# Seven block products instead of eight in the first MLP matmul, and a scheduler that keeps TensorE's array shape

## The chip, the cores and the metric

The kernel runs on one core of a Trainium2 chip, whose engines work side by side: TensorE (PE, with PEld for its weight loads), VectorE (DVE), ScalarE (ACT), GpSimd (POOL), and SyncE (SP), which issues the DMA transfers. The metric is the device time of one execution in microseconds, as the median of several runs; lower is better.

## The reference

One layer of a bidirectional RWKV-7 / GLA backbone for 256 context tokens and 2048 latent tokens of width 1024: a modulated RMSNorm, an input projection, two recurrent mixers, an output projection with a gated residual, and then what the change touches:

```python
    x = x + gt1 * o
    h = _rmsnorm(x, p['norm2_g']) * (1.0 + sc2) + sh2
    f = jnp.square(jax.nn.relu(h @ p['mlp_w1'])) @ p['mlp_w2']
    x = x + gt2 * f
    return x, new_states
...
    y_prompt = _rmsnorm(xp, final_norm_g)
    y_sample = _rmsnorm(xs, final_norm_g)
```

`mlp_w1` is 1024 x 4096 and `mlp_w2` 4096 x 1024, in float32. The gate `gt2` has one row for the context tokens and one for the latent tokens.

## The kernel before

Every large float32 product is made of three fast ones: an operand is split into a high part (ScalarE casts it) and a low part (VectorE subtracts the high part), and `mm3` issues high x high, high x low and low x high into one PSUM bank. A "triple" below is such a group.

The kernel has three stages. `proj` makes the input projection, with small matmuls of other array shapes between its triples (rows with `hh`, `hl`, `w_hi`, `w_lo` are the triples; rows `Q`, `K` belong to the GLA heads). `mixers` runs the scans. `tail` makes the output projection, the second norm and the MLP.

In each stage the program first records its instructions in a `Plan`; then `Plan.order` and `Plan.lay` set the order in which they are emitted on each engine. A recorded operation has a cost in the plan's own units, and its urgency is the cost of the longest chain behind it. `lay` goes through time, takes for each engine the most urgent operation that is ready, and hands out PSUM banks and work tiles as they come free. All emitted instructions carry the line number of that one loop (L534 in the profile before), so tiles are told apart by name and not by line.

The tail works on 18 units of 128 tokens, in the order of `UNITS`: units 9 and 10 hold the context tokens. `Tail.unit` makes the output projection of a unit (tiles `woh`, `wol`, and `h2h`, `h2l` for the mixer output), adds the residual, stores it (`d_x`), normalises and transposes it into `h2`. The split `h2` of nine units lies in SBUF in `h2h` and `h2l`; six of the eight blocks of units 9 to 16 and all of unit 17 go there directly, and the rest through DRAM (`d_h`) and `reload`.

`mlp(u0)` is called for units 9 to 17 and then for 0 to 8. Each pass has 16 groups (`gi`) of 256 hidden columns. A group loads two blocks of 128 columns of `mlp_w1` (tile `w1r`, split into `woh`, `wol`) and the matching rows of `mlp_w2` (`w2r`); makes for each 128 hidden columns and each 384 tokens a product over 8 blocks of the inner dimension, 24 matmuls of 384 columns into a bank `ps_1`; takes it through ReLU, square and split (`rr`); and multiplies with `mlp_w2`, 6 matmuls of 512 columns into a bank `ps_2` per 128 tokens and half width, which VectorE adds to `acc`. From group `PRE` = 13 on the gate is applied: `acc` is multiplied by `gt`, the residual is added, and the last two groups multiply their products by the gate before adding. In group 15 the final norm follows and the rows are stored.

The names `woh`, `wol` in the MLP's rows are the weights and hidden values, since all of these share those tiles.

## Time and profile before

| what | value |
|---|---|
| median of 3 runs | 3704.69 us (3702.34 to 3711.63) |
| profiled execution | 3709.88 us, span 3708.2 us |
| mean granted clock of TensorE | 0.963 |
| input projection | 0 to about 1280 us |
| mixers | about 1280 to 1810 us |
| units of the tail | about 1830 to 2085 us |
| MLP | about 2085 us to the end |
| DMA moved | 411.47 MB |

Times are microseconds unless marked ns. A row of the timeline gives start, duration, engine, line, operation, output <- inputs, shape and count, and in brackets the idle time before it and what ended it. A row of groups gives count, busy time, mean ns of one, and the idle time before. Matmuls overlap their successors, so a matmul's price is the distance between starts. A form such as 128*64 is the part of the array that a matmul uses.

### The profile page before, as it was taken

What the parts mean: (1) busy time and instruction counts of PE and PEld (TensorE: products, weight loads), DVE (VectorE), ACT (ScalarE), POOL (GpSimd) and SP (SyncE); (2) the same over time, 40 slices, a digit from 0 to 9 for tenths busy, and PEclk for the clock granted to TensorE, in tenths of its full rate; (3) what the DMA queues carried; (4) which work ended last, traced back from release to release, by engine and by line L of the source; (5) the groups of instructions that cost most, each with busy time, mean ns of one, the idle gap of its engine ahead of it and who ended that gap; (6) DMA issues with size and microseconds to landing.
All of it is one profiled execution on the core that took longest, in us unless ns stands there. A gap on an engine that the chain in (4) does not pass through costs nothing.

```text
span 3708.2 us, 74382 instructions
## 1 busy us (share of the span) xinstructions
PE 3504.4 (95%) x28927; PEld 3104.1 (84%) x28927; DVE 2249.8 (61%) x4991; ACT 1871.6 (50%) x4264; POOL 200.7 (5%) x500
## 2 busy tenths in 40 slices
PE   6999999999999779999699999999999999999998
PEld 4989888977888668888587899999999899999997
DVE  2665778756888778788487534334447734444357
ACT  5566857775568567788567622222223422222222
POOL 1111002200011210100000000000000000000000
PEclk8999999999999889899799999999999999999999
DMA  5356335532245655565688411111114311111122
GB/s 170 110 152 172 103 84 167 145 107 56 62 129 160 181 159 168 154 193 164 168 250 248 146 40 46 35 40 46 46 43 136 130 34 46 46 46 40 46 70 101
DMA packets 504207, 411.47 MB, mean 111 GB/s; under 512 B 87761, under 2 KB 458926, under 8 KB 503854
## 3 DMA queue, kind: packets, MB, share of 16 engines
q1 hardware_dynamic: 503854, 406.71, 37.6%
q8 instruction: 228, 3.74, 0.4%
q14 instruction: 125, 1.02, 0.1%
HBM read 287.03 MB, written 119.55 MB: 110 GB/s over the span
## 4 chain that ended last, share of the span: by engine, by line
PE 46%; DMA 2%; DVE 1%; ACT 1%; issue 0%; DVEq 0%; SPq 0%; ACTq 0%
PE ps L534 46%; DVE acc L534 1%; DMA hf<-d_h 0%; ACT hf L534 0%; DMA xb<-in_w_out_dram 0%; DVE xb L534 0%; DMA xa<-in_x_sample_dram 0%; DVE h2l L534 0%; DMA d_h<-hf 0%; DMA xb<-in_x_sample_dram 0%; DMA acc<-in_x_prompt_dram 0%; DMA xa<-in_x_prompt_dram 0%; ACT xb L534 0%; ACT h2h L534 0%; DVE gf L534 0%
## 5 line engine op out<-in xcount | busy, mean ns | idle before, releaser
L534 DVE TENSOR_TENSOR acc<-acc,ps 128x512 f32<-128x512 f32 x468 | 319.8, 688 | 504.0 <-PE ps L534 503.5
L534 PE MATMUL ps<-hh,w_hi 128*128 128x384 f32 (+3 forms) x1736 | 594.2, 342 | 5.2 <-ACT w_hi L534 3.9
L534 PE MATMUL ps<-hh,w_lo 128*128 128x384 f32 (+3 forms) x1736 | 548.7, 316 | 0.9 <-DVE w_lo L534 0.9
L534 PE MATMUL ps<-hl,w_hi 128*128 128x384 f32 (+3 forms) x1736 | 549.0, 316 | 0.0
L534 ACT ACTIVATE rr<-ps 128x384 f32<-128x384 f32 x192 | 94.4, 492 | 869.2 <-PE ps L534 861.5
L534 PE MATMUL ps<-h2l,woh 128*128 128x384 f32 x1536 | 516.4, 336 | 0.6 <-DVE h2l L534 0.4
L534 PE MATMUL ps<-h2h,woh 128*128 128x384 f32 x1536 | 513.9, 335 | 0.9 <-ACT h2h L534 0.9
L534 PE MATMUL ps<-h2h,wol 128*128 128x384 f32 x1536 | 514.1, 335 | 0.0
L534 PE MATMUL ps<-woh,wol 128*128 128x512 f32 x1152 | 456.2, 396 | 0.0
L534 PE MATMUL ps<-wol,woh 128*128 128x512 f32 x1152 | 454.0, 394 | 0.0
L534 PEld LDWEIGHTS ps<-hh,w_hi 128*128 128x128 f32 (+1 forms) x1736 | 328.4, 189 | 39.1 <-issue 10.3
L534 PEld LDWEIGHTS ps<-hl,w_hi 128*128 128x128 f32 (+1 forms) x1736 | 329.0, 190 | 2.9 <-DVE hl L534 0.4
L534 PEld LDWEIGHTS ps<-hh,w_lo 128*128 128x128 f32 (+1 forms) x1736 | 327.9, 189 | 3.4 <-DVE w_lo L534 1.7
L534 PEld LDWEIGHTS ps<-h2l,woh 128*128 128x128 f32 x1536 | 288.3, 188 | 23.3 <-DVE h2l L534 1.6
L534 PEld LDWEIGHTS ps<-h2h,woh 128*128 128x128 f32 x1536 | 288.4, 188 | 21.2 <-ACT h2h L534 1.6
L534 PE MATMUL ps<-woh,woh 128*128 128x512 f32 x774 | 301.1, 389 | 0.5 <-ACT woh L534 0.5
L534 PEld LDWEIGHTS ps<-h2h,wol 128*128 128x128 f32 x1536 | 288.3, 188 | 0.0
L534 DVE TENSOR_TENSOR wol<-rr,woh 128x384 fp32r<-128x384 f32 x192 | 103.7, 554 | 267.4 <-ACT woh L534 267.4
L534 PEld LDWEIGHTS ps<-woh,wol 128*128 128x128 f32 x1152 | 215.9, 187 | 46.7 <-DVE wol L534 0.9
L534 PEld LDWEIGHTS ps<-wol,woh 128*128 128x128 f32 x1152 | 215.9, 187 | 31.2
L534 ACT CAST woh<-rr 128x384 fp32r<-128x384 f32 x192 | 95.7, 515 | 201.4 <-PE ps L534 198.4
L534 PEld LDWEIGHTS ps<-woh,woh 128*128 128x128 f32 x774 | 145.4, 188 | 21.5 <-ACT woh L534 0.8
(296 smaller groups left out, 6735.7 us busy)
## 6 DMA issues: line engine op xcount, KB each, us to landing
w_raw<-in_w_in_dram SPq DMA_DIRECT2D x72, 512.0 KB
w1r<-in_mlp_w_dram SPq DMA_DIRECT2D x64, 512.0 KB
w2r<-in_mlp_w_dram SPq DMA_DIRECT2D x64, 512.0 KB
BK<-d_bk SPq DMA_DIRECT2D x36, 512.0 KB
AR<-d_ar SPq DMA_DIRECT2D x72, 256.0 KB
acc<-d_yo SPq DMA_DIRECT2D x36, 512.0 KB
w_raw<-in_ada_w_dram SPq DMA_DIRECT2D x32, 512.0 KB
d_ar<-s SPq DMA_DIRECT2D x56, 256.0 KB
```

What stands on the lines that cost most here:

```text
L534: getattr(getattr(self.nc, eng), method)(*[at(x) for x in args], **{k: at(x) for k, x in kw.items()})
```

## The change

Two things are changed.

**The MLP.** Its passes are three, over units 0 to 5, 12 to 17 and 6 to 11, 768 tokens each. All of `h2` goes through DRAM. Per group the first product is seen as a 2 x 2 block product: `mlp_w1`'s 256 columns in two halves, its 1024 rows in two halves, the tokens in two halves of 384. The Strassen-Winograd scheme replaces its eight block products by seven, each of 12 matmuls of 384 columns (4 blocks of the inner dimension, 3 each). `reload` forms the seven operands from `h2` once a pass: four blocks as loaded, and t1, t2, t3 and one further difference, each split high and low into `h2h`, `h2l`; VectorE and GpSimd share this. For the first pass it runs in two halves, since three of the operands lie where the output projection's weights were. `blocks` forms the four weight sums in place in `w1r` and in `s1`, splits seven operands, and adds the products in SBUF (tile `q`) before ReLU, square and split. In the two passes with a single gate row, `mlp_w2`'s rows are multiplied by the gate and the residual is loaded into `acc` at the start. The pass over units 6 to 11 has both gate rows and keeps the old scheme; it is last. PSUM turns of the tail change from three and two to five and three for `ps_1` and `ps_2`.

**The scheduler.** Each TensorE operation has an array shape (rows and columns rounded up to 32, 64 or 128). Where the most urgent ready one has another shape than the last one emitted, `lay` takes a ready one of the same shape whose urgency is less than `PW` = 2.0 behind, if its tiles are free. This holds in all three stages.

```diff
+PW = 2.0
...
-BK_TAIL = [2, {"ps_t": 3, "ps_h": 1, "ps_m": 3, "ps_1": 3, "ps_2": 2}]
+BK_TAIL = [2, {"ps_t": 3, "ps_h": 1, "ps_m": 3, "ps_1": 5, "ps_2": 3}]
...
             i = heapq.heappop(can[e])[1]
+            if e == "tensor" and self.shape[i] != shape:
+
+                for x in sorted(y for y in can[e] if y[0] < -prio[i] + PW and self.shape[y[1]] == shape):
+                    new = [y for y in self.held[x[1]].values() if y.ap is None]
+                    if not short(new) and all(min(idle[y.kind.name])[0] <= t for y in new):
+                        can[e].remove(x)
+                        can[e].append((-prio[i], i))
+                        heapq.heapify(can[e])
+                        i = x[1]
+                        break
...
-        self.h = [tp.tile([128, 8, 1152], F32R, name=f"h2{x}") for x in "hl"]
+        self.h = [tp.tile([128, 7, 4, 384], F32R, name=f"h2{x}") for x in "hl"]
...
-            k0 = 4 * i
-            k1 = k0 + 4 if u == 17 else min(k0 + 4, 8 - MR) if u >= 9 else k0
...
-            for k in range(k1, k0 + 4):
-                nc.sync.dma_start(out=d.h2[128 * k:128 * k + 128, us], in_=hf[:, k - k0])
+            for j in range(4):
+                k = 4 * i + j
+                nc.sync.dma_start(out=d.h2[128 * k:128 * k + 128, us], in_=hf[:, j])
...
+        def both(k, i, x):
+            hi, lo = [y[:, i, k] for y in self.h]
+            nc.scalar.copy(hi, x)
+            eng = nc.gpsimd if i in (1, 5, 6) else nc.vector
+            eng.tensor_tensor(out=lo, in0=x, in1=hi.bitcast(F32), op=ALU.subtract)
+        for k in range(4):
+            b11, t3, b22, b21 = load(k, 0, 0), load(k, 0, 1), load(k, 1, 1), load(k, 1, 0)
+            t1 = self.next(b)
+            TT(out=t1, in0=t3, in1=b11, op=ALU.subtract)
+            both(k, 0, b11)
+
+            t2 = self.next(b)
+            TT(out=t2, in0=b22, in1=t1, op=ALU.subtract)
+            nc.gpsimd.tensor_tensor(out=t3, in0=b22, in1=t3, op=ALU.subtract)
+            both(k, 2, t2)
+            both(k, 1, b21)
+            both(k, 3, t3)
+            if not first:
+                TT(out=b21, in0=b21, in1=t2, op=ALU.subtract)
+                both(k, 4, t1)
+                both(k, 5, b21)
+                both(k, 6, b22)
...
+        def part(w, b):
+            wh, wl = self.next("w1")
+            split(g, wh, wl, w)
+            ps = self.ps.tile([128, 512], F32, name="ps_1")[:, 0:384]
+            for k in range(4):
+                mm3(g, ps, wh[:, k], wl[:, k], self.h[0][:, b, k], self.h[1][:, b, k], k == 0, k == 3)
+            return ps
...
+        u1 = self.next("u")
+        nc.scalar.copy(u1, part(a11, 0))
+        TT(out=s1, in0=a21, in1=a22, op=ALU.add)
+        TT(out=a21, in0=a11, in1=a21, op=ALU.subtract)
+        TT(out=a11, in0=s1, in1=a11, op=ALU.subtract)
+        u2 = add("u", u1, part(a11, 2))
+        out(0, 0, add("r", u1, part(a12, 1)))
+        u3 = add("u", u2, part(a21, 3))
+        p5 = part(s1, 4)
+        out(1, 1, add("r", u3, p5))
+        TT(out=u2, in0=u2, in1=p5, op=ALU.add)
+        TT(out=s1, in0=a12, in1=a11, op=ALU.subtract)
+        out(1, 0, add("r", u3, part(a22, 5)))
+        out(0, 1, add("r", u2, part(s1, 6)))
...
+        if one:
+            self.gate(grp[0], 1)
+            for i in turn:
+                residual(i, acc[i])
...
+                if one:
+                    TT(out=raw, in0=raw, in1=self.gt, op=ALU.mult)
...
-        t.mlp(9)
-        for k in range(8):
-            for u0 in (0, 3, 6):
-                t.reload(k, u0, 3)
-        t.mlp(0)
+        for u0 in (0, 12, 6):
+            t.reload(u0, u0 == 0)
+            t.mlp(u0)
```

Three places show how the emitted order moves. The first is PE in the input projection, in the last third of its triples. Before:

```order
L534 MATMUL ps_120<-Q_188,K_214 64x64 x4
L534 MATMUL ps_119<-hh,w_hi_200 128x384
L534 MATMUL ps_119<-hl,w_hi_200 128x384
L534 MATMUL ps_119<-hh,w_lo_202 128x384
L534 MATMUL ps_125<-Q_189,K_215 64x64 x4
```

With the change, at the same place among the triples:

```order
L562 MATMUL ps_121<-hl,w_hi_199 128x384
L562 MATMUL ps_121<-hh,w_lo_201 128x384
L562 MATMUL ps_126<-Q_189,K_215 64x64
L562 MATMUL ps_124<-Q_188,K_214 64x64 x4
L562 MATMUL ps_126<-Q_189,K_215 64x64 x3
L562 MATMUL ps_121<-hh,w_hi_199 128x384
L562 MATMUL ps_121<-hl,w_hi_199 128x384
L562 MATMUL ps_121<-hh,w_lo_201 128x384
L562 MATMUL ps_123<-hh,w_hi_200 128x384
```

Two small groups of one shape, each of which stood alone between triples, now stand together. The second place is DVE in a steady MLP group. Before, accumulations and splits alternate, with one split of 1024 columns per weight block:

```order
L534 TENSOR_TENSOR wol_21711<-w1r,woh_21710 128x1024
L534 TENSOR_TENSOR wol_21713<-rr,woh_21712 128x384
L534 TENSOR_TENSOR acc_21717<-acc_21717,ps_21740 128x512
L534 TENSOR_TENSOR acc_21717<-acc_21717,ps_21735 128x512
L534 TENSOR_TENSOR acc_21717<-acc_21717,ps_21738 128x512
L534 TENSOR_TENSOR acc_21717<-acc_21717,ps_21739 128x512
```

With the change (`q` with `ps` is a sum of block products, `s` and `w1r` without a low part are weight sums, `w2r` with `gt` is the gate):

```order
L562 TENSOR_TENSOR wfl<-w1r,wfh 128x512 x3
L562 TENSOR_TENSOR wfl<-s_21714,wfh 128x512
L562 TENSOR_TENSOR s_21714<-w1r 128x512
L562 TENSOR_TENSOR acc<-acc,ps_21727 128x512
L562 TENSOR_TENSOR acc<-acc,ps_21729 128x512
L562 TENSOR_TENSOR acc<-acc,ps_21733 128x512
L562 TENSOR_TENSOR q<-q,ps_21730 128x384
L562 TENSOR_TENSOR wfl<-w2r,wfh 128x1024
L562 TENSOR_TENSOR wfl<-w1r,wfh 128x512
L562 TENSOR_TENSOR q<-q,ps_21728 128x384
```

Between the accumulations there are now sums out of PSUM and of weights, and more and smaller splits. The third place is DVE where the first pass meets the second. It stands there now:

```order
L562 TENSOR_TENSOR q<-xb,q 128x384
L562 TENSOR_TENSOR xa<-q 128x384
L562 TENSOR_TENSOR q<-q 128x384
L562 TENSOR_TENSOR q<-q,xa 128x384
L562 TENSOR_TENSOR h2l<-xa,h2h 128x384
L562 TENSOR_TENSOR acc<-acc,ps_21728 128x512
L562 TENSOR_TENSOR acc<-acc,ps_21734 128x512
L562 TENSOR_TENSOR acc<-acc,ps_21733 128x512
L562 TENSOR_TENSOR wfl<-w2r,wfh 128x1024
L562 TENSOR_TENSOR h2l<-q,h2h 128x384 x2
```

Rows of `q`, `xa`, `xb` without `ps` are operand differences, and `h2l` rows are their splits. Before, where the two passes met, only splits stood in this place, between gate products:

```order
L534 TENSOR_TENSOR h2l<-hf,h2h 128x384
L534 TENSOR_TENSOR acc_21714<-acc_21714,xb 128x512
L534 TENSOR_TENSOR wol_21713<-rr,woh_21712 128x384 x2
L534 TENSOR_TENSOR wol_21711<-w2r,woh_21710 128x1024
L534 TENSOR_TENSOR h2l<-hf,h2h 128x384 x2
L534 TENSOR_TENSOR wol_21711<-w1r,woh_21710 128x1024
```

More of the change, by code (lines that the diff above doesn't have):

```diff
@@ L445, in lay, with short @@
         step = -1 if back else 1
+        def short(new):
+            for x in new:
+                if len(idle[x.kind.name]) <= (0 if x.n == turn[x.kind.name] else x.kind.spare):
+                    return x
         cur, self.nsw = None, 0
+        shape, self.nshape = None, 0
         engs = ("tensor", "vector", "scalar", "gpsimd", "sync")
@@ L472, in lay @@
             i = heapq.heappop(can[e])[1]
+            if e == "tensor" and self.shape[i] != shape:
[7 more added lines that the diff above has]
+                        break
             new = [x for x in self.held[i].values() if x.ap is None]
-            lack = [x for x in new if len(idle[x.kind.name]) <= (0 if x.n == turn[x.kind.name] else x.kind.spare)]
+            lack = short(new)
             if lack:
-                stuck[lack[0].kind.name].setdefault(lack[0].n, []).append(i)
+                stuck[lack.kind.name].setdefault(lack.n, []).append(i)
                 continue
@@ L500, in lay @@
             t = max(t, ready[i])
+            if e == "tensor":
+                if self.shape[i] != shape:
+                    pass
+                    self.nshape += 1
+                shape = self.shape[i]
             free[e] = t + busy
@@ L1571, in __init__ @@
         halves = lambda x: [x[:, 0:512], x[:, 512:1024]]
+        cut = [q[:, 384 * i:384 * i + 384] for i in range(8)]
         self.rings = {
[L1573 to L1576 removed]
@@ new lines, in reload, with load @@
+    def reload(self, u0, first=False):
+        g = self.g
+        nc, TT = g.nc, g.nc.vector.tensor_tensor
+        b = "b0" if first else "b"
+        def load(k, i, j):
+            r0, c0 = 128 * (4 * i + k), 128 * (u0 + 3 * j)
+            x = self.next(b)
+            nc.sync.dma_start(out=x, in_=g.d.h2[r0:r0 + 128, c0:c0 + 384])
+            return x
+        def both(k, i, x):
[19 more added lines that the diff above has]
+                both(k, 6, b22)
+        b = "b1"
+        for k in range(4) if first else ():
+            b11, t1, b22, t4 = load(k, 0, 0), load(k, 0, 1), load(k, 1, 1), load(k, 1, 0)
+            TT(out=t1, in0=t1, in1=b11, op=ALU.subtract)
+            both(k, 4, t1)
+            TT(out=t4, in0=t4, in1=b22, op=ALU.subtract)
+            both(k, 6, b22)
+            TT(out=t4, in0=t4, in1=t1, op=ALU.add)
+            both(k, 5, t4)
@@ new lines, in blocks, with add, out @@
+    def blocks(self, gi):
+        g = self.g
+        nc, TT = g.nc, g.nc.vector.tensor_tensor
+        w1 = g.a["mlp_w1"].rearrange("l (k p) n -> p (l k) n", p=128)
+        raw = self.next("w1r").rearrange("p (k n) -> p k n", k=8)
+        nc.sync.dma_start(out=raw, in_=w1[:, :, 256 * gi:256 * gi + 256])
+        a11, a12, a21, a22 = [raw[:, 4 * j:4 * j + 4, 128 * i:128 * i + 128] for i in range(2) for j in range(2)]
+        s1 = self.next("s1").rearrange("p (k n) -> p k n", k=4)
+        def part(w, b):
[5 more added lines that the diff above has]
+            return ps
+        def add(nm, x, y):
+            r = self.next(nm)
+            TT(out=r, in0=x, in1=y, op=ALU.add)
+            return r
+        fs = [self.next("f") for _ in range(2)]
+        def out(i, j, r):
+            cs = slice(384 * j, 384 * j + 384)
+            nc.scalar.activation(out=r, in_=r, func=AF.Relu)
+            nc.scalar.activation(out=r, in_=r, func=AF.Square)
+            split(g, fs[i][0][:, cs], fs[i][1][:, cs], r)
+        u1 = self.next("u")
[12 more added lines that the diff above has]
+        out(0, 1, add("r", u2, part(s1, 6)))
+        return fs
@@ new lines, in final @@
+    def final(self, u0, i):
+        g = self.g
+        nc, x, tok = g.nc, self.acc[i], 128 * UNITS[u0 + i]
+        ss = self.sm.tile([128, 2], F32, name="ss")
+        for c in range(2):
+            cs = slice(512 * c, 512 * c + 512)
+            nc.scalar.activation(out=self.rings["t"][0], in_=x[:, cs], func=AF.Square, accum_out=ss[:, c:c + 1])
+        nc.vector.tensor_tensor(out=ss[:, 0:1], in0=ss[:, 0:1], in1=ss[:, 1:2], op=ALU.add)
+        rs = rstd(nc, self.sm, ss[:, 0:1], float(D), 1e-6, "xr")
+        nc.vector.scalar_tensor_tensor(out=x, in0=x, scalar=rs, in1=self.gf, op0=ALU.mult, op1=ALU.mult)
+        if tok < TP:
+            nc.sync.dma_start(out=g.out["y_p"][tok:tok + 128, :], in_=x)
+        else:
+            nc.sync.dma_start(out=g.out["y_s"][tok - TP:tok - TP + 128, :], in_=x)
@@ L1726, in mlp @@
                 ws.append((vh, vl))
[L1727 to L1740 removed]
+            for i in turn:
+                if not one and gi > PRE and i in new:
+                    self.gate(grp[i], 1)
                 ts_ = slice(128 * i, 128 * i + 128)
[L1742 removed]
                 for c in range(2):
```

112 lines of the change are left out of this document (41 added, 71 removed).

## The prediction

> **What bounds the kernel now.** I read the page's busy shares and chain first, then the stretches, then the groups and single matmuls of the MLP.
>
> ```profile
> PE 3504.4 (95%) x28927; PEld 3104.1 (84%) x28927; DVE 2249.8 (61%) x4991; ACT 1871.6 (50%) x4264; POOL 200.7 (5%) x500
> ...
> 2113.74 761.59 PE ps L534 x3828
> ...
> 2896.69 785.38 PE ps L534 x3953
> ...
> 1830.00:2085.00 255.00, 240.11 (x1146) 196.12 (x1147) 194.30 (x412) 174.81 (x514) 0.00 (x0) 0.95 0.83 238
> 2085.00:2840.00 755.00, 751.80 (x3793) 679.91 (x3792) 329.09 (x464) 202.31 (x367) 0.00 (x0) 1.00 0.18 55
> 2840.00:2900.00 60.00, 59.61 (x302) 53.87 (x302) 46.77 (x88) 30.60 (x73) 0.00 (x0) 1.00 0.49 157
> 2900.00:3640.00 740.00, 740.00 (x3727) 670.17 (x3726) 335.36 (x476) 192.42 (x350) 0.00 (x0) 1.00 0.18 56
> ```
>
> After the page's first line stand two links of the chain of waits, then the windows (length; busy time of PE, PEld, DVE, ACT, POOL; granted clock; DMA share; GB/s). From 2085 us to the end the kernel is the MLP, and PE is the chain there: 761.59 and 785.38 us without a foreign link. PE is busy all 740 us of the second pass at clock 1.00. Even where the passes meet (2840 to 2900) it is busy 59.61 of 60, while DVE works 46.77. A matmul less here is therefore time less, as long as nothing else grows into the bound.
>
> A busy matmul overlaps its successor, so its price is the distance of starts:
>
> ```profile
> 2299.71 0.33 PE L534 MATMUL ps<-h2h,wol 128*128 128x384 f32 x1
> ...
> 2303.00 0.39 PE L534 MATMUL ps<-woh,woh 128*128 128x512 f32 x1
> ...
> 2304.39 0.33 PE L534 MATMUL ps<-h2h,woh 128*128 128x384 f32 x1
> ```
>
> Nineteen 384-column matmuls from 2299.71 to 2303.00: 0.173 us each. Six of 512 columns to 2304.39: 0.232 us. The MLP has 4608 and 3456 of them: 798 + 801 = 1599 us, which is the span from 2085 to the last matmul (about 3691) but for 7 us.
>
> **Term 1, the products.** A group of 256 hidden columns and 768 tokens took 8 block products of 12 matmuls, and takes 7. In 48 such groups (3 passes of 16) that is 48 x 12 = 576 matmuls of 384 columns fewer: 576 x 0.1732 = **-99.8 us**. The second MLP product keeps its 3456. PE per group becomes 84 x 0.1732 + 72 x 0.2315 = 31.2 us.
>
> **Term 2, VectorE in the steady groups.** The missing product is paid in sums and in more weight splits:
>
> ```profile
> L534 DVE TENSOR_TENSOR acc<-acc,ps 128x512 f32<-128x512 f32 x180 | 123.0, 688 | 199.9 <-PE ps L534 199.7
> ...
> L534 DVE TENSOR_TENSOR wol<-rr,woh 128x384 fp32r<-128x384 f32 x60 | 32.4, 554 | 97.6 <-ACT woh L534 97.6
> ...
> L534 DVE TENSOR_TENSOR wol<-w2r,woh 128x1024 fp32r<-128x1024 f32 x20 | 24.5, 1223 | 4.3 <-ACT woh L534 4.3
> ```
>
> A group now issues on DVE 12 accumulations (688 ns), 7 weight splits and 4 weight sums of 512 columns (I price them at 688), 7 sums out of PSUM and 4 splits of 384 (554), 2 splits and, in two passes of three, 2 gate products of 1024 (1223): 8.3 + 7.6 + 6.1 + 4.9 = 26.8 us of 31.2. So DVE goes from 335 of 740 us, 45%, to about 86% in the MLP, and still ends inside PE's time. Its queue has 4.4 us to spare per group, and PSUM's eight banks let PE run ahead of it. Steady groups: **+0 us**, with 0 to 10 over the whole as bounds. ScalarE comes to some 13 us per group. The weights are read three times instead of twice; at a DMA share of 0.18 now, half as much again leaves the queue far from full.
>
> **Term 3, where passes meet.** There are two such places now instead of one, each with a whole reload of h2: per k, DVE forms t1, t2 and a difference and splits four of the seven operands, POOL makes one difference and three splits. Counted in the built order from the last product of a pass's last group to the first of the next pass's second group: at the first meeting DVE has 43 instructions of 384 columns, 31 of 512, 12 of 1024 and 15 of one column (0.15 us), PE 96 and 117 matmuls. DVE: 43 x 0.554 + 31 x 0.688 + 12 x 1.223 + 2 = 62 us; PE: 16.6 + 27.1 = 43.7 us. At the second: 43, 38, 7, 13 against 144 and 111 matmuls: 61 against 50.6 us. Here DVE is late, and PE waits for it. Instructions that follow without a gap cost a little less than their listed time:
>
> ```profile
> 2043.06 1.29 DVE L534 TENSOR_TENSOR xa<-xa,acc 128x512 f32<-128x512 f32 x2 [1.24 <-DMA xa<-in_x_sample_dram]
> ...
> 3582.40 2.73 DVE L534 TENSOR_TENSOR acc<-acc,ps 128x512 f32<-128x512 f32 x4 [1.80 <-PE ps L534]
> ```
>
> Two from SBUF: the second started 0.60 us after the first (0.87 of 0.69); four from PSUM: 0.68 each. With 0.87 on all but the 18 and 19 accumulations out of PSUM the DVE sums are 12.4 + 0.87 x 49.6 = 56 and 13.1 + 0.87 x 47.9 = 55 us: the lower bounds of the waits are 12 and 4 us. The upper bounds come from POOL:
>
> ```profile
> 608.55 0.42 DVE L534 TENSOR_TENSOR s<-s 128x256 f32<-128x256 f32 x1
> 608.65 0.92 POOL L534 TENSOR_TENSOR s<-s 128x256 f32<-128x256 f32 x1
> 608.89 0.96 DVE L534 SCALAR_TENSOR_TENSOR s<-s,nkk 128x256 f32<-128x256 f32 x1
> 609.77 0.41 DVE L534 TENSOR_TENSOR s<-s,Ep 128x256 f32<-128x256 f32 x1
> ```
>
> While POOL's 256-column sum ran, DVE's instruction took 0.96 us where its like around it take 0.41 to 0.49: 0.5 us lost per POOL sum. A meeting has 16 POOL instructions of 384 columns; scaled by 1.5 that is up to 0.75 x 16 = 12 us of DVE. With it the waits are up to 30 and 22 us. I take **+20 and +12 us**.
>
> The Trainium skill (SBUF — State Buffer, Who interferes with whom) says that a VectorE instruction with two SBUF inputs contends with a GpSimd instruction that reads SBUF; the row agrees, and it speaks against this change, whose reload puts such instructions on both engines at once. By that rule in full the two waits would be 30 and 22, and the sum below 20 us later; without it 12 and 4.
>
> **Term 4, the seam from the units to the MLP.** Before, half of h2 stayed in SBUF and PE idled little:
>
> ```profile
> 2085.00:2100.00 15.00, 13.11 (x79) 12.17 (x78) 5.29 (x12) 14.24 (x33) 0.00 (x0) 1.00 0.59 207
> 2100.00:2115.00 15.00, 13.69 (x74) 12.17 (x72) 5.34 (x10) 5.85 (x13) 0.00 (x0) 1.00 0.35 116
> ```
>
> 3.2 us of 30. Now all of h2 goes through DRAM: units 9 to 17 issue 72 stores of 64 KB on SP instead of 16, and 16 loads of 192 KB come beside them, 7 MB more in a stretch that moves 255 us x 238 GB/s = 61 MB at a share of 0.83. That makes 0.92, still under one, and the first nine units, which always stored all their blocks, ran without a foreign link:
>
> ```profile
> 1853.23 101.37 PE ps L534 x485
> ```
>
> So the units cost nothing more. The first pass takes units 0 to 5, finished long before, and its operands 1 to 4 are formed under the later units, whose PE is busy 240 of 255 us. Operands 5 to 7 lie where the output weights were and come after the last unit: 3 x 4 operands, 8 of the POOL splits (8 x 1.1 x 1.5 us = 13 us by the POOL row below), beside four products (8 us), some 24 transposes and first accumulations. I take **+6 us**, bounds 0 and 20 (POOL's 13 us uncovered, and 7 for loads that come late).
>
> ```profile
> L534 POOL TENSOR_TENSOR s<-s 128x256 f32<-128x256 f32 x28 | 30.9, 1104 | 38.8 <-DVE s L534 32.6 <-PE ps L534 3.2 <-issue 2.9
> ```
>
> **Term 5, the last three groups.** The mixed pass (both gates) is last and keeps the old scheme: in group 13 12 products and sums of 1024 columns, in 14 and 15 12 more of 512.
>
> ```profile
> 3589.92 1.22 DVE L534 TENSOR_TENSOR acc<-acc,gt 128x1024 f32<-128x1024 f32 x1
> ...
> DVE acc L534 <- DMA gt<-d_mod: 4.1, 1, 4.1
> ```
>
> Group 13: 24.4 + 12 x 1.22 = 39 us of DVE against 31.2; group 14: 24.4 + 8.3 = 32.7; a gate load costs DVE up to 4.1 us once a change isn't covered. Before, 18 instead of 12 accumulations' PE time covered the same. **+10 us**, bounds 5 and 25.
>
> **Term 6, array shapes.** In the built order PE changes its array shape 703 times before the mixers and 572 now; in the mixers 279 and 264; in the tail never. A change's price:
>
> ```profile
> 521.59 0.34 PE L534 MATMUL ps<-hl,w_hi 128*128 128x384 f32 x1
> 521.77 0.34 PE L534 MATMUL ps<-hh,w_lo 128*128 128x384 f32 x1
> 522.03 0.46 PE L534 MATMUL ps<-Q,K 128*64 128x64 f32 x8
> 522.42 0.44 PE L534 MATMUL ps<-hh,w_hi 128*128 128x384 f32 x1
> 522.71 0.34 PE L534 MATMUL ps<-hl,w_hi 128*128 128x384 f32 x1
> ...
> 498.57 0.86 PE L534 MATMUL ps<-Q,K 128*64 128x64 f32 x16
> 499.36 0.44 PE L534 MATMUL ps<-hh,w_hi 128*128 128x384 f32 x1
> ```
>
> The matmul before the change lasts 0.26 instead of 0.173, the first one after the return 0.29: 0.2 us a round trip. The small group itself costs 0.39 for 8 and 0.79 for 16, so nothing more is hidden in it. 146 changes x 0.1 = 14.6 us, if PE is the bound:
>
> ```profile
> 0.00:1280.00 1280.00, 1195.26 (x9267) 1038.83 (x9268) 888.17 (x2328) 851.82 (x1850) 156.13 (x448) 0.96 0.45 128
> ```
>
> It is busy 93% there; I take two thirds, **-10 us**, bounds -15 and +5 (a less urgent matmul ahead may delay a chain that ends in a wait).
>
> **Sum.** -99.8 + 0 + 20 + 12 + 6 + 10 - 10 = -62 us. The profiled execution took 3709.9 us (span 3708.2), 5 more than the median of 3704.7. From the median: **3643 us**.
>
> **The rivals.** (a) *Hidden as before.* The old meeting shows 59.61 of 60 us with DVE at 78%; if the new ones hide at the pitch and POOL costs nothing, terms 3 to 5 shrink to about 13: -99.8 + 13 - 13, 3605 us. For it: matmuls of the second product are free to be moved there. Against: the counts above, where DVE has more than PE. (b) *All at the upper ends:* 30 + 22 + 20 + 25 and no gain from shapes: -3 us against the old time, if steady groups are clean; half-way there, 3673 us. For it: three engines chained per operand. (c) *VectorE becomes the bound, slower than before.* In the quoted row 199.9 us of idle stand before 180 accumulations: 1.1 us each, waiting for PE. If in the new groups 19 such waits for PSUM cost DVE 0.4 us each that it can't catch up, a group takes 26.8 + 7.6 = 34.4 us, and 48 x 3.2 = 154 us are added: 3643 + 154 = 3797. It decides from 32.5 us a group on, where the gain is gone. Against: DVE waits there because it is early; once it is the late one, such a wait vanishes. The change not doing what it says is no rival: the built order has 7488 MLP matmuls for 8064.
>
> A waiting PE may also lose its clock: the granted clock was 0.52 from 1830 to 1845 us, after an idle of 24 us, but 0.94 or more around short idles.
>
> ```profile
> 1830.00:1845.00 15.00, 9.42 (x28) 6.77 (x29) 11.31 (x25) 9.33 (x27) 0.00 (x0) 0.52 1.00 300
> 1995.00:2010.00 15.00, 10.72 (x52) 8.24 (x51) 12.18 (x27) 11.08 (x34) 0.00 (x0) 0.94 0.90 247
> ```
>
> Waits of 20 us in small pieces are nearer to the second row, so I add nothing.
>
> **How the numbers follow.** Forecast 0.56 (3620 to 3665), (a) 0.20, (b) 0.19, (c) 0.05. The range 3608 to 3682 leaves (c), a half of (b)'s far side and the deeper part of (a) outside. 0.3% of the time is 11 us, about what a measurement tells from no change: slower 0.04 (most of (c)), same 0.03 (the far end of (b) and the edge of (c)), faster 0.93.
>
> **What would show it.** Right: MLP matmuls at the same 0.173 and 0.232 us apart, 576 fewer; PE without gaps in steady groups and DVE near 80 to 86%; PE idle of 10 to 30 us at each meeting, ended by DVE or POOL writes of h2; the first 1830 us some 10 us shorter. Wrong: PE idle ended by DVE in every group (c); PE whole across the meetings (a); a first part that is longer, from chains that the shape rule held back.

## The result, and the profile after

The change takes 3674.43 us (median of 4 runs, 3673.79 to 3679.7) against 3703.89 us for the kernel before (3702.34 to 3711.63): ratio 0.9919, 95% interval 0.9902 to 0.9937. A second comparison gave 0.9909 (0.9896 to 0.9923). So it is some 30 us faster; the forecast was 62 faster. The time lies inside the range, and half of the expected gain is missing.

The products are gone as forecast. The first line and TensorE's busy time on the page of the change:

```profile
span 3672.7 us, 74545 instructions
...
PE 3408.1 (93%) x28351; PEld 3013.9 (82%) x28351; DVE 2729.4 (74%) x5859; ACT 2074.6 (56%) x4652; POOL 250.9 (7%) x548
```

28351 matmuls instead of 28927: 576 fewer. In the timeline of the change their pitch is the old one: 12 of 384 columns from 2154.40 to 2156.48 are 0.173 us each, 21 of 512 from 2140.04 to 2144.83 are 0.228:

```profile
2140.04 0.40 PE L562 MATMUL ps<-wfh 128*128 128x512 f32 x1
...
2144.83 0.39 PE L562 MATMUL ps<-wfh 128*128 128x512 f32 x1
...
2154.40 0.33 PE L562 MATMUL ps<-h2h,wfh 128*128 128x384 f32 x1
...
2156.48 0.33 PE L562 MATMUL ps<-h2h,wfh 128*128 128x384 f32 x1
```

What was given back is read from stretches of the tail (length; busy time of PE, PEld, DVE, ACT, POOL; granted clock; DMA share; GB/s). The change:

```profile
1826.75:2150.00 323.25, 285.33 (x1313) 230.65 (x1314) 238.21 (x477) 202.84 (x574) 19.06 (x16) 0.92 0.83 240
1826.75:2050.00 223.25, 206.11 (x964) 166.54 (x965) 173.91 (x368) 147.41 (x446) 9.20 (x8) 0.95 0.91 256
2050.00:2150.00 100.00, 79.22 (x351) 64.12 (x350) 64.30 (x110) 55.43 (x129) 9.86 (x8) 0.86 0.64 203
2590.00:2690.00 100.00, 90.14 (x414) 77.88 (x413) 91.64 (x152) 52.28 (x115) 19.37 (x16) 0.95 0.45 150
3095.00:3200.00 105.00, 95.80 (x452) 84.59 (x451) 92.02 (x154) 54.60 (x118) 20.48 (x16) 0.93 0.37 122
3560.00:3658.00 98.00, 94.27 (x449) 82.21 (x447) 89.13 (x143) 38.06 (x77) 0.00 (x0) 0.98 0.30 102
...
2700.00:3100.00 400.00, 400.00 (x2003) 361.13 (x2003) 312.58 (x491) 157.87 (x288) 0.00 (x0) 1.00 0.22 68
```

The kernel before, its units and their seam to the MLP:

```profile
1831.76:2155.00 323.24, 306.90 (x1493) 256.30 (x1494) 219.42 (x451) 203.95 (x574) 0.00 (x0) 0.96 0.71 205
1831.76:2040.00 208.24, 195.46 (x921) 159.15 (x922) 161.63 (x350) 140.10 (x427) 0.00 (x0) 0.94 0.90 254
2040.00:2155.00 115.00, 111.44 (x574) 97.16 (x573) 57.79 (x102) 63.85 (x147) 0.00 (x0) 1.00 0.35 116
```

TensorE's loss in a stretch is its length less busy time x granted clock: length less busy is waiting, the rest is slow matmuls. (A clock of two digits leaves 1.5 us of doubt in 300.)

| stretch of the change | waiting | slow matmuls | lost | lost before | forecast of the difference |
|---|---|---|---|---|---|
| units and seam, to 2150 us | 37.9 | 22.8 | 60.7 | 28.6 | +6 |
| first meeting, 2590 to 2690 | 9.9 | 4.5 | 14.4 | 0.4 | +20 |
| second meeting, 3095 to 3200 | 9.2 | 6.7 | 15.9 | none | +12 |
| last groups, 3560 to 3658 | 3.7 | 1.9 | 5.6 | 0 | +10 |
| steady groups (2700 to 3100) | 0 | 0 | 0 | 0 | 0 |

The losses differ by 32 + 14 + 16 + 6 = 68 us; 99.8 less 68 is 32. The tail, from its first transposition to the end of the span, got 30.5 us shorter (1876.4 to 1845.9), which is the whole measured gain. So most of what is missing lies at the seam, which lost 26 us more than was forecast. By the rows, 28 of its 32 us fall behind the units: from 2050 to 2150 us the change loses 100 less 79.22 x 0.86, 31.9 us, where before lost 115 less 111.44 x 1.00, 3.6. Up to 2050 it is 27.5 us against 24.5.

### The profile page after: what moved, and what is told of

Its sections match the earlier page's. It is cut to its first block, busy times and chain, and to the rows that moved or that the text cites. A ratio compares the mean times of both kernels' runs of the same rounds, so it can differ in the third digit from the quotient of the medians.

```text
span 3672.7 us, 74545 instructions
## 1 busy us (share of the span) xinstructions
PE 3408.1 (93%) x28351; PEld 3013.9 (82%) x28351; DVE 2729.4 (74%) x5859; ACT 2074.6 (56%) x4652; POOL 250.9 (7%) x548
## 5 line engine op out<-in xcount | busy, mean ns | idle before, releaser
L562 PE MATMUL ps<-wfh 128*128 128x512 f32 x1296 | 516.7, 399 | 31.8 <-ACT wfh L562 17.0
L562 PE MATMUL ps<-wfh,wfl 128*128 128x512 f32 x1296 | 517.0, 399 | 5.0 <-DVE wfl L562 4.8
L562 PE MATMUL ps<-h2l,wfh 128*128 128x384 f32 (+1 forms) x1488 | 511.5, 344 | 8.9 <-DVE h2l L562 8.9
L562 PE MATMUL ps<-h2h,wfh 128*128 128x384 f32 (+1 forms) x1488 | 513.4, 345 | 3.2 <-ACT wfh L562 2.2
L562 PE MATMUL ps<-wfl,wfh 128*128 128x512 f32 x1296 | 514.0, 397 | 0.0
L562 PE MATMUL ps<-h2h,wfl 128*128 128x384 f32 (+1 forms) x1488 | 512.5, 344 | 1.2 <-DVE wfl L562 1.1
L562 PEld LDWEIGHTS ps<-wfh 128*128 128x128 f32 x1296 | 247.3, 191 | 77.5 <-ACT wfh L562 19.5
L562 PEld LDWEIGHTS ps<-h2l,wfh 128*128 128x128 f32 x1488 | 281.9, 189 | 29.6 <-DVE h2l L562 11.4
L562 PEld LDWEIGHTS ps<-h2h,wfh 128*128 128x128 f32 x1488 | 282.1, 190 | 22.8 <-ACT wfh L562 3.2
L562 PEld LDWEIGHTS ps<-h2h,wfl 128*128 128x128 f32 x1488 | 281.6, 189 | 9.0 <-DVE wfl L562 2.8
```

What stands on the lines that cost most here:

```text
L562: getattr(getattr(self.nc, eng), method)(*[at(x) for x in args], **{k: at(x) for k, x in kw.items()})
```

## The experiments

All ratios are to the kernel before, run on the same chip. "Tail" is the span less the start of the tail's first transposition, in the one profiled execution; "seam" is the loss as above, from there to about 2150 us. Some expectations count losses over other stretches or in another way (44.7 us for the old tail, 41 us of slow matmuls at the seam); the runs are compared by this table.

| run | ratio (95% interval) | span | tail | seam |
|---|---|---|---|---|
| before | 1 | 3708.2 | 1876.4 | 28.6 |
| the change | 0.9919 (0.9902 to 0.9937) | 3672.7 | 1845.9 | 60.7 |
| the change again (e19) | 0.9909 (0.9896 to 0.9923) | 3667.5 | 1843.7 | 58.0 |
| e1 without the rule | 0.9922 (0.9904 to 0.9941) | 3665.1 | 1846.4 | 59.1 |
| e2 the rule alone | 1.0007 (0.9995 to 1.0019) | 3701.2 | 1875.9 | 28.7 |
| e3 third staging buffer | 0.9916 (0.9901 to 0.9931) | 3667.8 | 1842.4 | 57.8 |
| e4 reload without POOL | 0.9905 (0.9884 to 0.9925) | 3669.6 | 1841.5 | 58.9 |
| e5 merged stores | 0.9921 (0.9903 to 0.9939) | 3660.6 | 1837.2 | 50.5 |
| e6 landing 6 us | 0.9847 (0.9822 to 0.9871) | 3649.2 | 1822.4 | 37.7 |
| e7 no late stores | 0.9877 (0.9859 to 0.9895) | 3658.5 | 1829.8 | 44.7 |
| e8 light early reload | 0.9910 (0.9894 to 0.9925) | 3660.9 | 1839.4 | 52.5 |
| e9 light meetings | 0.9848 (0.9817 to 0.9879) | 3642.8 | 1817.7 | 60.2 |
| e10 before, landing 6 us | 1.0081 (1.0054 to 1.0108) | 3730.4 | 1908.0 | 21.0 |
| e11 landing 6 us, no POOL | 0.9848 (0.9821 to 0.9876) | 3647.1 | 1820.4 | 42.4 |
| e12 landing 10 us | 1.0304 (1.0280 to 1.0329) | 3811.7 | 1985.8 | 76.0 |
| e16 landing 6 us, units only | 0.9880 (0.9861 to 0.9900) | 3658.2 | 1833.1 | 49.8 |
| e17 and the last groups | 0.9865 (0.9851 to 0.9879) | 3653.6 | 1831.9 | 45.8 |
| e18 and no POOL | 0.9847 (0.9833 to 0.9860) | 3639.5 | 1820.4 | 44.4 |
| e20 and the first reload | 0.9846 (0.9827 to 0.9864) | 3634.7 | 1820.5 | 46.8 |
| e21 and merged stores | 0.9836 (0.9817 to 0.9854) | 3640.3 | 1822.5 | 47.1 |

### The scheduler rule

e1 is the change without it:

```diff
-PW = 2.0
+PW = 0.0
```

> The change without its scheduler rule (the allowance is 0 instead of 2, so the plan picks by urgency alone); the MLP with seven products stays. Account of the two traces: the rule is worth 5 us (the tail began 5.0 us earlier), so 3679 us. The prediction's step (10 us) would give 3684. If the rule also reordered something in the tail to its good, more than 3684.

e2 is the kernel before with `short`, the shapes and the rule in `lay`, as in the change's diff, and nothing else.

> The kernel before with the scheduler rule alone; MLP, buffers and PSUM shares as before. Account of the traces: 5 us off 3704, so 3699 us. The prediction's step: 10 off, 3694. If a less urgent matmul put ahead delays a chain: 3704 or more.

Both miss: without the rule the change is as fast (0.9922 against 0.9919 and 0.9909), and the rule alone gives 1.0007. The 5 us by which the change's tail began earlier were the spread between executions. The timeline's row of the tail's first transposition, of before, the change, e1 and e2 in this order:

```profile
1831.76 1.36 PE L534 MATMUL ps<-ident,acc 128*128 128x128 f32 x4 [24.39 <-ACT acc L534]
```

```profile
1826.75 1.35 PE L562 MATMUL ps<-ident,acc 128*128 128x128 f32 x4 [24.23 <-ACT acc L562]
```

```profile
1818.66 1.36 PE L562 MATMUL ps<-ident,acc 128*128 128x128 f32 x4 [25.27 <-ACT acc L562]
```

```profile
1825.26 1.36 PE L562 MATMUL ps<-ident,acc 128*128 128x128 f32 x4 [25.08 <-ACT acc L562]
```

Without the rule it began at 1831.8 and 1818.7, with it at 1826.8 and 1825.3. Up to there the kernels with the rule are one program, and among the spans and tails of the table (span less tail) its start lies between 1814.2 (e20) and 1828.7 (e7). The tail's length is the steadier measure: 1845.9, 1843.7 and 1846.4 us for three executions of the same MLP.

The rule does save TensorE's time. From 0 to 1810 us, for the same 19711 matmuls at a mean granted clock of 0.94, the profile shows it busy 1635.3 to 1637.5 us in three executions with the rule (e2, the change, e19) and 1656.0 to 1661.3 in three without (before, e1, e10). That is some 20 us less, and these stages don't end earlier for it.

### The meetings

e9 takes work out of both meetings (`kk` picks the block that a product reads):

```diff
+        self.kk = lambda b, k: k if first else 0
-        for k in range(4):
+        for k in range(4 if first else 1):
             b11, t3, b22, b21 = load(k, 0, 0), load(k, 0, 1), load(k, 1, 1), load(k, 1, 0)
```

> The reloads of the second and third pass form one of four k blocks of the seven operands, and the products use it in the place of all four (output not the reference's); the first pass is whole, TensorE's work is the same. At each of the two meetings VectorE loses 21 instructions of 384 columns (0.47 us each in sequence, 10 us) and GpSimd 12 (about 0.8 us of VectorE's time each, 10 us). If VectorE's sum sets the meetings, as the prediction's third step has it, both waits (16.5 and 15.4 us with the slow matmuls behind them) all but vanish: 25 to 32 us off the tail's 1846.0, 1814 to 1821, ratio to before 0.983 to 0.985. If the products' chain (a product, its sum, ScalarE's square, the split, the second product) or the loads set it: 0 to 10 us off.

It came out as expected, 0.9848, the tail 28.2 us shorter. Two stretches of e9 that hold the two meetings:

```profile
2560.00:2660.00 100.00, 96.20 (x479) 85.79 (x478) 84.00 (x146) 47.73 (x104) 5.52 (x4) 1.00 0.42 139
3060.00:3160.00 100.00, 99.53 (x496) 89.17 (x495) 88.73 (x150) 52.22 (x109) 5.00 (x4) 1.00 0.33 113
```

TensorE loses 3.8 and 0.5 us instead of 14.4 and 15.9, and the clock stays at 1.00. In the change VectorE had not a moment free there:

```profile
2610.00:2620.00 10.00, 8.46 (x38) 6.61 (x37) 10.00 (x18) 6.03 (x16) 4.49 (x5) 1.00 0.63 190
2620.00:2630.00 10.00, 6.09 (x24) 4.71 (x24) 10.00 (x20) 6.35 (x16) 4.72 (x4) 0.88 0.06 18
2630.00:2640.00 10.00, 8.76 (x37) 8.15 (x37) 10.00 (x15) 5.27 (x16) 2.42 (x2) 0.78 0.73 275
2640.00:2650.00 10.00, 6.83 (x28) 5.29 (x28) 9.94 (x22) 5.42 (x14) 0.00 (x0) 0.91 0.92 320
```

e9 takes loads and ScalarE's and GpSimd's part away with VectorE's, so by itself it doesn't tell them apart; these rows do. At the second meeting it is the same: VectorE is busy all of 3130 to 3150 us, and TensorE's longest wait there, 5.1 us, is ended by VectorE's `acc`. Between the two products that the prediction counted from at the first meeting VectorE is busy 59.9 of 60.5 us, where 62 were counted. So VectorE's sum sets the meetings. Its rows also show GpSimd in its way (timeline of the change, VectorE and GpSimd):

```profile
2606.43 0.55 DVE L562 TENSOR_TENSOR q<-xa 128x384 f32<-128x384 f32 x1
...
2607.05 1.27 POOL L562 TENSOR_TENSOR xa<-xb,xa 128x384 f32<-128x384 f32 x1 [0.97 <-DVE q L562]
2607.36 1.37 DVE L562 TENSOR_TENSOR q<-xb,q 128x384 f32<-128x384 f32 x1
...
2609.95 0.55 DVE L562 TENSOR_TENSOR q<-q 128x384 f32<-128x384 f32 x1
```

1.37 us beside a GpSimd instruction, 0.55 without. e4 therefore gives VectorE all of it:

```diff
-            eng = nc.gpsimd if i in (1, 5, 6) else nc.vector
+            eng = nc.vector
...
-            nc.gpsimd.tensor_tensor(out=t3, in0=b22, in1=t3, op=ALU.subtract)
+            TT(out=t3, in0=b22, in1=t3, op=ALU.subtract)
```

> All differences and splits of the reload on VectorE, none on GpSimd. If the two contend as the trace suggests (a VectorE instruction of 384 columns took 1.37 instead of 0.55 us while GpSimd worked, about 0.8 us lost per GpSimd instruction, while the same work costs VectorE 0.47 us in sequence): each meeting of two passes gets 0.33 x 16 = 5 us shorter on VectorE, and with the clock behind it the time goes to 3664 to 3670 us. If GpSimd's help is real and the longer instructions cost nothing on the path: 16 x 0.47 = 7.5 us more at each of the three reloads, 3689 to 3697.

The rival is excluded: doing GpSimd's instructions on VectorE as well cost nothing. The gain is small: the tail is 4.4 us shorter than in the change (2.2 than in its repetition), and the timed ratio can't tell it from the change's.

### The seam: buffer, issues, bytes, work

Between 2030 and 2130 us of the change several things are late. SyncE's issues, VectorE's wait for `yo`, and what follows on ScalarE and TensorE (timeline; in brackets the idle time before and what ended it):

```profile
2039.67 1.26 SPq L562 DMA_DIRECT2D acc<-d_yo  x2
...
2042.66 5.70 SPq L562 DMA_DIRECT2D q<-d_h  x2
...
2049.28 1.29 DVE L562 TENSOR_TENSOR acc<-acc 128x512 f32<-128x512 f32 x2 [4.07 <-DMA acc<-d_yo]
...
2057.76 0.62 ACT L562 CAST wfh<-gf 128x512 fp32r<-128x512 f32 x1 [1.84 <-DVE gf L562]
...
2058.43 0.80 PE L562 MATMUL ps<-wfh 128*128 128x512 f32 x1 [7.19 <-ACT wfh L562]
...
2127.02 0.81 ACT L562 ACTIVATE q<-ps,modT,A 128x128 f32<-128x128 f32 x2 [7.84 <-DMA d_h<-q]
```

The two `yo` loads were issued by 2040.93, and VectorE could use them at 2049.28, 8.4 us later. TensorE's longest wait, 7.19 us, is ended by a cast of ScalarE that had waited for VectorE behind this; ScalarE itself had stood 3.63 us, until 2049.40, for a store of h2 to land. At 2127.02 ScalarE had stood 7.84 us before a staging buffer whose store hadn't landed, with the MLP's casts queued behind it. From 1860 to 2110 us VectorE waited for nine such pairs of `yo` loads in the change; they landed 6.0 to 8.4 us after their issue, 7.4 in the mean. In the kernel before there were eight, with 6.0 to 8.0 us, 6.5 in the mean. Four runs follow, each aimed at one cause.

e3, a third staging buffer (paid for with one of the first reload's five buffers; t1 and t2 are then formed in place, not shown):

```diff
-            "hf": halves(q[:, 2048:3072]),
+            "hf": [q[:, 1536 + 512 * i:2048 + 512 * i] for i in range(3)],
...
-            "b0": cut[0:5],
+            "b0": cut[0:4],
```

> A third staging buffer of 512 columns for h2 on its way to DRAM (two before); the columns come from the first pass's reload buffers (four instead of five; t1 and t2 are formed in place). Bytes moved and engine work are the same. Theory A (ScalarE, in order, stands before a staging buffer whose store has not landed, 7.8 us at 2127, and the MLP's own casts and activations wait behind it): the waits of TensorE between 2050 and 2150, 20.7 us, fall by 7 to 10, and 6 to 12 us go with the slow matmuls after them: 3662 to 3668 us. Theory B (the 7 MB more are the cost, the transfers being full in this stretch) and theory C (the engine work of the early reload is the cost): no change, 3672 to 3677.

e5, fewer issues for the same bytes (h2's layout in DRAM and the reload's loads follow, not shown):

```diff
-            for j in range(4):
-                k = 4 * i + j
-                nc.sync.dma_start(out=d.h2[128 * k:128 * k + 128, us], in_=hf[:, j])
+            nc.sync.dma_start(out=d.h2.rearrange("p (k t) -> p k t", k=8)[:, 4 * i:4 * i + 4, us], in_=hf)
```

> Each unit stores h2 with 2 transfers of 256 KB instead of 8 of 64 KB (h2 lies in DRAM as 128 partitions by 8 blocks, so that four blocks are one transfer); bytes and packet sizes are the same. SyncE issues 108 transfers less, at some 0.42 us each. Counted from the tail's first transposition to the end of the span, before took 1876.4 us and the change 1846.0. Theory D (SyncE's queue, which issues in order and between 1900 and 2050 us either issues or waits for a producer, makes the units' loads late): 5 to 15 us off, 1831 to 1841, ratio to before 0.988 to 0.991. Theory B (bytes): no change, 1843 to 1849.

e7, fewer bytes (and with them 96 fewer issues, and no wait of a staging buffer for these stores):

```diff
+                if u < 6:
                     nc.sync.dma_start(out=d.h2[128 * k:128 * k + 128, us], in_=hf[:, j])
...
-            r0, c0 = 128 * (4 * i + k), 128 * (u0 + 3 * j)
+            r0, c0 = 128 * (4 * i + k), 128 * 3 * j
```

> Units 6 to 17 don't store h2 at all and the second and third pass load the columns of the first (the output is not the reference's for their tokens); all work on the engines stays. 96 stores, 6.3 MB, are gone from the units. Theory B: 6.3 MB at 0.26 MB per us is 24 us of full transfers, so 15 to 24 us off the tail, 1822 to 1831 us. Theory A and D: the same sign, but no more than their own part, 5 to 10 us. If the early reload's work is the cause: no change.

e8, less early reload (the products read by `kk`, as in e9):

```diff
+        self.kk = lambda b, k: 0 if first and b < 4 else k
-        for k in range(4):
+        for k in range(1 if first else 4):
```

> The first pass forms only one of four k blocks of its operands 1 to 4 under the units and multiplies it in the place of all four (output not the reference's); 12 loads of 192 KB, 24 VectorE, 12 ScalarE and some POOL instructions are gone from the units, the stores of h2 stay, and TensorE's work is the same. If the early reload (its loads in SyncE's queue and its work on three engines) is the cause of the 9 us lost more in the units and of a part of the seam: 10 to 20 us off, 1826 to 1836 us. If the stores are: within 3 us of 1846, or up to 6 off for its 2.4 MB.

A third staging buffer, at the price of a reload buffer, brought nothing (0.9916; seam 57.8). Fewer issues shortened the profiled tail by 8.7 us, but not the timed runs (0.9921): inconclusive. The light early reload gave 6.5 us of tail and 0.9910, little. Without 6.3 MB of stores the ratio is 0.9877 and the tail 16.1 us shorter, as expected if bytes count; since issues and staging waits go with them, and e5 leaves open what issues are worth, the bytes' own share isn't shown alone. The stretch of e7:

```profile
1828.65:2150.00 321.35, 294.31 (x1387) 244.21 (x1388) 248.18 (x493) 210.70 (x587) 19.22 (x16) 0.94 0.78 227
```

321.35 less 294.31 x 0.94 is 44.7 us of loss instead of 60.7: 16 us, half of the 32 in question.

### The seam: when the plan expects a transfer

The plan that sets the order counts a transfer as landed 1.7 us after its issue, plus 0.0014 us per element of a partition: 4.6 us for a `yo` load of 2048, 1.9 for a store of h2. The loads above took 6.0 to 8.4 us for the former. e6 plans the tail with 6 instead of 1.7 (`landing`, which starts at 1.7); the work is the same:

```diff
-            d = (0.63, 1.7 + 0.0014 * n)
+            d = (0.63, self.landing + 0.0014 * n)
...
+        plan.landing = 6.0
         t.weights()
```

> The tail's plan is made with transfers that land 6 us after their issue instead of 1.7 (plus the same part by size); the work is the same, only the order on the engines moves. If the seam's loss comes from an order that expects transfers too early (ScalarE and VectorE stand before work whose data is under way while other work is ready): 5 to 15 us off, the tail at 1831 to 1841 us. If the bytes or the engines' work set it: within 3 us of 1846.

> The kernel before, with its tail planned for transfers that land 6 us after their issue. If the early order is a loss of the new seam alone: 3700 us as before (its tail 1876 us, of which 44.7 us were lost up to 2150). If the old tail lost by it as well: its 44.7 us could fall by 10 to 15 us, 3686 to 3691, and the later landing would then explain only the rest of the 24 us that it gave the change.

> The change, planned with a landing of 10 us instead of 1.7 (6 gave 0.9847). The VectorE waits for yo in the change were 14.0 us in 7 pieces, the longest 4.1; with 6 they are gone, so 10 should bring nothing more at the seam: within 5 us of the landing of 6. If loads still come late at the meetings (where the later landing left 23 and 21 us), 5 to 10 us less; if the plan fetches so early that buffers are held, 5 to 10 us more.

e6 gives more than the expected 5 to 15 us: 0.9847, its interval below the change's, the tail 23.5 us shorter. The stretches of e6: units and seam, two meetings, last groups.

```profile
1826.82:2150.00 323.18, 300.52 (x1436) 248.33 (x1437) 257.80 (x505) 212.54 (x595) 20.48 (x16) 0.95 0.85 248
...
2570.00:2670.00 100.00, 80.57 (x379) 69.78 (x378) 93.54 (x151) 52.51 (x114) 23.77 (x15) 0.91 0.42 141
3070.00:3180.00 110.00, 98.00 (x449) 85.85 (x448) 94.86 (x153) 55.41 (x119) 21.01 (x16) 0.92 0.36 121
3530.00:3633.00 103.00, 102.33 (x502) 90.47 (x500) 92.76 (x152) 40.19 (x80) 0.00 (x0) 1.00 0.29 97
```

The seam loses 37.7 us instead of 60.7, the last groups 0.7 instead of 5.6; the meetings lose more, 26.7 and 19.8 instead of 14.4 and 15.9. VectorE's waits for `yo` between 1860 and 2110 us (sum, times, longest) in the change, in e6 and in the kernel before:

```profile
DVE acc L562 <- DMA acc<-d_yo: 18.3, 9, 4.1
```

```profile
DVE acc L562 <- DMA acc<-d_yo: 0.7, 2, 0.4
```

```profile
DVE acc L534 <- DMA acc<-d_yo: 10.8, 8, 2.7
```

The loads didn't get faster: the two that VectorE still waited for in e6 landed 6.9 and 7.5 us after their issue, at a DMA share of 0.85 instead of 0.83. Hardly anything waits for them now. But it is no cure in itself. The kernel before gets slower by it (1.0081). Its stretches, units and seam, and the old meeting:

```profile
1822.43:2150.00 327.57, 316.08 (x1561) 267.14 (x1562) 226.74 (x461) 211.12 (x588) 0.00 (x0) 0.97 0.71 206
2770.00:2930.00 160.00, 143.50 (x681) 126.97 (x681) 112.22 (x180) 59.77 (x133) 0.00 (x0) 0.95 0.42 141
```

Its seam loses 21.0 us instead of 28.6, so a late transfer had cost the old tail something too; its meeting, which lost 0.4, now loses 23.7. Another 16 us go at its end: 7.6 in the last 120 us before the last matmul, where before lost nothing, and 8 behind it (25.1 us to the end of the span instead of 17.0). And with 10 us the change itself goes to 1.0304, far outside all that was expected of it: TensorE is no longer whole even in steady groups of e12 (part of its second pass):

```profile
2900.00:3100.00 200.00, 188.41 (x916) 167.97 (x916) 143.99 (x223) 72.44 (x126) 0.00 (x0) 0.97 0.20 64
```

All of TensorE's waiting there, 11.6 us, is ended by VectorE's splits of weights. So the number helps at the seam, where transfers are late, and harms the MLP, where they take a share of 0.2; by which choices of the plan it harms isn't shown. The next runs use it by place.

### The landing by place, and the best version

e16 plans with 6 us for the units and 1.7 from the first reload on; e17 sets it to 6 again from the last pass's group 13 on; e18 adds e4's edit to e17; e11 is e6 with e4's edit; e20 is e18 with 6 us for the first reload too; e21 adds e5's edit to e20. e16's edit, and behind it e17's:

```diff
+        plan.landing = 6.0
         t.weights()
         for u in range(18):
             t.unit(u)
+        plan.landing = 1.7
...
+            if gi == PRE and not one:
+                nc.landing = 6.0
```

> The change, planned with a landing of 6 us for the transfers of the weights' loads and the units alone (stores, yo, gbs, x), 1.7 us from the first reload on. The later landing for the whole tail gave the seam 23.6 us, took 6.6 us at the last groups, and lost 6 and 5 us more at the two meetings (23 and 21 against 16.5 and 15.4). If the seam's loss comes from the units' own transfers that the old plan expects too early: the gain of the seam stays and the meetings are as in the change, the tail at 1820 to 1826 us, ratio to before 0.984 to 0.987. If the reload's loads are the late ones: the tail at 1840 to 1846, ratio 0.990 to 0.992.

> As the run before, and with 6 us again from the last pass's group 13 on (gate and residual loads and the outputs). TensorE's loss at the last groups, 6.6 us in the change and 0 with the later landing throughout, goes: the tail some 5 to 7 us below the run before, 1814 to 1820 us, ratio 0.982 to 0.985. If that loss goes by another part of the plan: as the run before, within 2 us.

> As the run before, and with the reload's differences and splits on VectorE alone. With the early landing this gave the two meetings 4.6 us together (1.3 and 3.3) and the tail 4.5: the tail at 1810 to 1816 us, ratio 0.981 to 0.984. If it counts for nothing once the order is another (as with the later landing throughout): within 2 us of the run before.

> The change, planned with a landing of 6 us, and with the reload's differences and splits on VectorE alone. If the two causes are apart (order at the seam, GpSimd's contention with VectorE), the gains add: 24 + 4 us off the change, ratio to before 0.983 to 0.985, the tail at 1816 to 1820. If VectorE is the bound now at the seam too, where the later landing has closed the gaps: no gain over the later landing alone, 0.985 to 0.988.

> As the run e18 (landing of 6 us for the units and from the last pass's group 13 on, no POOL work in the reload), and the first reload's loads planned with 6 us too. With the units alone the seam up to 350 us after the tail's start lost 28 us in waits and 38 in slow matmuls (38 and 41 in the change), with 6 us throughout 22 and 33. If the first reload's loads hold the other half: some 10 us off e18's tail of 1820.4, 1810 to 1814 us, ratio 0.981 to 0.984. If the difference came from the passes behind: within 3 us of e18.

> As the run before, and with h2 stored by 2 transfers of 256 KB a unit instead of 8 of 64 KB (in the change alone: tail 8.8 us shorter in the profiled execution, timed ratio unchanged). If SyncE's issues still make loads late: 3 to 9 us off the run before. If the later landing has taken that away: within 3 us.

> The change itself once more, beside the three others on one chip: ratio to before 0.990 to 0.994, the tail at 1846 us; its first part (before the tail) is expected to differ by up to 5 us from the profile shown, as that of the kernels without and with the scheduler rule did.

With the units alone (e16) the ratio is 0.9880, and the seam gets back 11 us of the 23: between its two cases. So a share of the late landing lies in the units' transfers. Its meetings, planned with 1.7 us again, lose 15 and 14 us, as in the change. e17's tail is only 1.2 us shorter (0.9865): TensorE's waiting in the last 120 us before its last matmul goes from 3.7 to 0.2 us, as expected, but the time behind that matmul grows from 13.6 to 16.9. e18 goes to 0.9847 with a tail 11.5 us shorter. That is more than the 4.5 us that the same edit was worth in the change, though the tail stays above the range forecast; in e11 beside e6 it counts for nothing. e20 comes out in its second case: the first reload's loads don't hold the rest (1820.5 against 1820.4). So does e21. Five versions (e6, e11, e18, e20, e21) end within 0.0012 of each other, 0.9836 to 0.9848, all with an interval below the change's; their own intervals overlap, so none of them is shown to be the best. e21, the lowest, took 3643.9 us (3641.23 to 3646.41) against 3704.28 for the kernel before, about twice the change's gain.

## Why the prediction was wrong

**Term 1, the products: right.** 576 matmuls fewer at the old pitch, and no loss elsewhere in the steady groups.

**Term 2, steady groups at nothing: right.** TensorE is busy 400.00 of 400 us at clock 1.00. VectorE is at 312.58 of 400, 78%, below the 86% counted: 24.4 us of a group's 31.2. The rival by which VectorE becomes the bound is dead.

**Term 3, the meetings: right in sum, and in its cause.** 14.4 + 15.9 = 30 us instead of 20 + 12, and e9, with the rows in which VectorE has no moment free, shows that it is VectorE's work. But of these 30 only 19 are waits; 11 are slow matmuls behind them, which the prediction left out. By waits alone the term was 13 us too high: that the sum fits is in part luck.

**Term 4, the seam: this is the step that failed.** It was put at +6 with an upper bound of 20, and was +32. The working said that the DMA share becomes 0.92, "still under one", and that "the units cost nothing more". The share came out (0.91 up to 2050 us), and up to there TensorE lost only 3 us more than before. The other 28 came in the 100 us behind, at a mean share of 0.64, where TensorE waited 20.8 us, each time for VectorE or ScalarE. Two things were wrong with the working. The bytes were counted short: the page of transfers from 1830 to 2150 us has, for the change and for before,

```profile
DMA packets 77367, 76.30 MB, mean 238 GB/s; under 512 B 4531, under 2 KB 70451, under 8 KB 77343
```

```profile
DMA packets 69610, 66.72 MB, mean 208 GB/s; under 512 B 3226, under 2 KB 63130, under 8 KB 69587
```

9.6 MB more instead of 7. In this stretch the change issues 35 loads of 192 KB from h2 where 16 were counted, since the second half of the first reload loads its blocks again, and six of 512 KB (`acc<-d_x`) for the residual, which weren't counted; eight loads from h2 and one of the residual that stood there before weren't taken off. And a mean share under one was taken to mean that nothing waits. At 0.91 the `yo` loads took 6.0 to 8.4 us, where the plan had ordered the engines for 4.6, and each engine works in its order. e6 (the same work with an order that expects them later, 23 of the 32 back) shows the part of the order; e7 (fewer bytes, with fewer issues, 16 of the 32 back) the part of the transfers. The two overlap, and 9 of the 32 us are still there in e6. The trace of before had a sign of it that was not read: VectorE's waits for `yo`, 10.8 us in 8 pieces at a share of 0.90.

**Term 5, the last groups:** 5.6 us instead of 10, beside 2 us less behind the last matmul (17.0 to 15.0 us to the end of the span). Right mechanism, size a half.

**Term 6, array shapes: wrong.** 10 us forecast, nothing measured (e1, e2). The price, read from a single row, was about right: TensorE is busy some 20 us less up to 1810 us with the rule, where 146 changes at 0.1 us make 14.6. But two thirds of it was put on the path without showing that TensorE sets the end of these stages, and by e1 and e2 it doesn't.

**The clock: wrong.** "I add nothing", said the prediction of a waiting TensorE. Around the first meeting (timeline of the change):

```profile
2626.54 0.44 PE L562 MATMUL ps<-h2l,wfh 128*128 128x384 f32 x1 [2.16 <-DVE h2l L562]
...
2628.28 0.69 PE L562 MATMUL ps<-h2l,wfh 128*128 128x384 f32 x1 [0.96 <-DVE h2l L562]
2628.77 0.53 PE L562 MATMUL ps<-h2h,wfl 128*128 128x384 f32 x1
...
2633.89 0.53 PE L562 MATMUL ps<-h2h,wfh 128*128 128x384 f32 x1
...
2634.69 0.34 PE L562 MATMUL ps<-h2h,wfh 128*128 128x384 f32 x1
```

Sixteen matmuls from 2628.77 to 2633.89 are 0.32 us apart instead of 0.173. In the stretches of the first table slow matmuls are 22.8 + 4.5 + 6.7 + 1.9 = 36 us, before 12: 24 us of the 68 lost are this. The Trainium skill (TensorE: Matmul & The Clock Gate, HAM oscillation — how this bites in real kernels) warns of idle gaps above about 3.4 us. The longest gap at this meeting was 2.16 us, so here shorter ones were enough.

In all: -99.8 (products) + 32 (seam) + 30 (meetings) + 6 (last groups) - 2 (behind the last matmul) + 0 (shapes) = -34, against -30.5 us of tail and -30 of measured time. Of the forecast's 32 missing us the seam holds 26 and the shapes 10, and the smaller terms give 8 back; the 4 left over lie within the rounding of the clock. The rival with all terms at their upper ends gave 3673, close to the time, but for another reason: the meetings and the end were below their upper ends, and the seam far above its own.

What stays open: which rule of the plan makes the meetings lose more with the later landing, in the change (30 to 47 us) as in the kernel before; whether e6's order is better at the seam for the expected landing alone, or also by chance, since any other number gives another order; where the other half of e6's gain at the seam comes from, since neither the units' transfers nor the first reload's hold it alone; and whether e5's shorter profiled tail is real.

## What to carry to other kernels

Here a stage at a mean DMA share of 0.9 couldn't take more transfers for nothing. In such a stage look for engines that already wait for a load there, and price the added bytes at the stage's own rate. Where a planner sets the order, compare its transfer times with the landing times in the trace, stage by stage; here the number that helped the full stage harmed the emptier ones. And price a wait of TensorE with the slow matmuls behind it, here 24 us of them for 44 us of added waits.
